# Convolution half of the output product on scaled fp16 parts: raw w_o rows, scales from squares

## The chip, the cores and the metric

The kernel runs on one core of a Trainium2 chip. A core has five engines that run their own instruction streams in order and meet at semaphores: TensorE (PE, matrix products), VectorE (DVE), ScalarE (ACT), GpSimd (POOL) and SyncE (SP). SP and POOL also issue the transfers (DMA) between the memory of the chip and the core; POOL's queue may convert or add on the way, SP's copies. The metric is the device time of one execution in microseconds (us).

## The reference

The program computes a two-layer encoder trunk on a sequence of 1024 rows of width 1024. Each layer has a mixer and a feed-forward part, each behind an RMS norm with a residual around it. The mixer has two halves of width 512, which one output matrix joins:

```python
h = _rmsnorm(x, g_mix[l])
p = h @ w_in[l]
...
y_att = softmax(q k / sqrt(96)) v          # 8 heads of 64, keys of 64 + 32 (rotary)
...
u = a * sigmoid(g)                          # gated half, 512 channels
u = silu(_layernorm(_dwconv(u, w_dw_conv, b_dw_conv), g_conv_ln, b_conv_ln))   # 31 taps
x = x + concatenate([y_att, u]) @ w_o[l]
...
x = x + gated_conv_ffn(_rmsnorm(x, g_ffn[l]), w_up[l], w_down[l])
```

The block is shortened from the reference; what matters here is the product with `w_o`. Its first half takes the attention output, its second half the output of the convolution module.

## The kernel before

Everything is held transposed: channels on the 128 partitions, the 1024 rows along the free axis, in two column halves of 512. To keep float32 precision, each operand of a product is split into an upper and a lower part (names end in `h` and `l`), and three matmuls per block (upper by upper, upper by lower, lower by upper) are added up in PSUM. In the feed-forward part and in the attention the parts are f16; in the projections and in the product with `w_o` they are float32r.

A layer runs in this order on PE:

- **Projection** (`project`). Sections of the product with `w_in` (`pg`, `pa` for the gated half, `pkv`, `pq`, `pkr`), then keys, queries and values. Beside it DVE works on the 31 taps of the convolution (`conv`, L1993), ACT on the gate sigmoids (L646), on copies for weights (`complete`, L200) and on products `far` for taps that a transfer adds up (L1999). A planner with a table of section times keeps a clock; `launch`, `work` and `supply` place evictions, taps and weight loads along it, and that fixes the order of each engine. `supply` loads a weight with a converting transfer on POOL's queue (the upper part), lets ACT write its negative (`complete`), and lets a second transfer add the source to it, which leaves the lower part. In layer 0 the rotary tables are computed at the same time, written out by two transfers and read back by eight `cos` and eight `sin` transfers on SP's queue (L670).
- **Scales** (`weight_squares`, `scales`). Near the end of the projection ACT takes sums of squares of the value weights (`vsq`) and of the gains (`sc`, L916); one small matmul (`sc0p`) adds them over partitions, and ten small DVE operations make powers of two from them.
- **Attention** (`attention`). 64 steps, each with scores `s`, exponentials `p` on ACT, a transposition `t`, the split `pt` (upper on ACT, lower on DVE) and the product `o`. An agenda, a list of functions by step number, adds other work: taps that are left (on ACT and POOL), the loads of the w_o tiles for the attention half from step 55 (`WO_AT`), the totals `lns` of the layer norm on POOL (from step `TOTAL_TIME`), the multiplies of `yt` by the softmax reciprocals (`LAST_MULT`, `Y_DELAY`), and the splits `ys` of the attention output (`ys_5l` on POOL).
- **Output product** (`wo_steps`, L1000). First `po<-ys`, the attention half, then `po<-us`, the convolution half; each is 8 blocks of output by 2 column halves by 4 tiles by 3 matmuls. `put(step, rank, f)` places loads, copies and evictions by step and by rank within it. The tiles of both halves come by converting and adding transfers on POOL's queue, 256 KB each. Layer norm and SiLU of the convolution run beside the first half; `close` (ACT) and `rest` (DVE) make the parts `us`. DVE adds the sums from PSUM to the residual (L1034, L1038).
- **Feed-forward part** (L1266, L1511), which the change does not touch.

Tiles come from pools of equal slots: 31 named `b`, 8 `m`, 3 `wr`, 8 `ws`. A load into a slot waits until the slot's last reader is done.

Of the kernel before, what the change touches and what calls it, by code (L numbers as in the profile page):

```python
# [9 lines left out]
F32 = mybir.dt.float32  # L10
F32R = mybir.dt.float32r
I32 = mybir.dt.int32
# [53 lines left out]
TOTAL_TIME = 59  # L66
Y_DELAY = 6
Y_LAST = 4
LAST_MULT = (60, 61)
WO_AT = 55  # L70
END_TURNS = 1
P_SCALE = 32768.0
# [64 lines left out]
class Encoder:  # L137
# [274 lines left out]
    def first_sections(self, l, supply):  # L412
# [14 lines left out]
        nc.scalar.activation(out=self.cp.tile([128, 1], F32, name="table"), in_=self.ones[:, 0:1], func=AF.Square)  # L427
# [83 lines left out]
        nc.gpsimd.tensor_copy(out=self.cp.tile([128, 1], F32, name="held"), in_=x[2][:, 0:1])  # L511
# [46 lines left out]
    def project(self, l, carry):  # L558
# [10 lines left out]
        qk = self.cp.tile([128, 8], F32, name=f"qk{l}", tag="qk", bufs=1)  # L569
        col = lambda i, n=1: qk[:, i:i + n]  # L570
# [290 lines left out]
        scales = {1: lambda: st.update(squares=self.weight_squares(l, w["v"])),  # L861
                  2: lambda: (st.update(scale=self.scales(l, st.pop("squares"))), score_scale())}
# [8 lines left out]
        coming, turning = list(starts.items()) + [("v", t + 6.0)], []  # L871
# [12 lines left out]
        gain_squares()  # L884
        launch(gate(0), -3)
# [21 lines left out]
        return u, conv, away, (qd, qrd, kd, krd), (kvs, w["v"], st["scale"]), heads  # L907

    def weight_squares(self, l, w):
        nc, par = self.nc, self.par[l]  # L910
        f = self.cp.tile([128, 20], F32, name=f"sc{l}", tag="sc", bufs=1)
# [4 lines left out]
        nc.scalar.activation(out=f[:, 8:16], in_=par[:, P_GFFN:P_GFFN + 8], func=AF.Square, accum_out=f[:, 2:3])  # L916
        return f
# [8 lines left out]
    def scales(self, l, f):  # L926
        nc = self.nc
        ps = self.bank(f"sc{l}p", (128, 3))
        nc.tensor.matmul(ps, self.ones, f[:, 0:3], start=True, stop=True)
        col = lambda i: f[:, i:i + 1]  # L930
        nc.vector.tensor_copy(out=f[:, 2:5], in_=ps)
        nc.vector.tensor_tensor(out=col(3), in0=col(2), in1=col(3), op=ALU.add)
        self.half_exponent(f[:, 5:7], f[:, 3:5])
        self.power(col(0), col(5), -1.0, 200.0)
        self.power(col(1), col(5), 1.0, 39.0)
        self.power(col(7), col(6), -1.0, 197.0)
        nc.vector.tensor_scalar(out=col(16).bitcast(I32), in0=col(6).bitcast(I32), scalar1=EXPONENT, scalar2=-20.0 * EXPONENT,
                                op0=ALU.mult, op1=ALU.add)
        nc.vector.tensor_copy(out=col(17), in_=col(16).bitcast(I32))
        nc.vector.tensor_scalar(out=f[:, 8:16], in0=self.par[l][:, P_GFFN:P_GFFN + 8], scalar1=col(7), scalar2=None, op0=ALU.mult)  # L940
        nc.vector.tensor_scalar(out=col(18), in0=col(17), scalar1=-2.0 ** 31, scalar2=None, op0=ALU.add)
        self.gs, self.back, self.nback = f[:, 8:16], col(17), col(18)
        return col(0), col(1)

    def layer(self, l, carry):
        with self.psum(f"mix{l}", ([f"w{i}" for i in range(3)], 1), 2):
            mixed = self.project(l, carry)
        with self.psum(f"attn{l}", 2, 4):
            casts, ready = {}, {}
            ahead = {WO_AT: lambda: [casts.update({m: self.wo_cast(l, m, 1)}) for m in range(4)],  # L950
                     **{58 + m: lambda m=m: ready.update({(1, m): self.complete(*casts.pop(m))}) for m in range(3)},
                     61: lambda: (ready.update({(1, 3): self.complete(*casts.pop(3))}), [casts.update({m: self.wo_cast(l, m, 1)}) for m in range(4, 8)])}
            begun = {"x": {}, "po": {}}
            begun["turn"] = lambda: ready.update({(1, m): self.complete(*casts.pop(m)) for m in range(4, 4 + END_TURNS)})
            conv, ys = mixed[1], self.attention(l, *mixed, ahead, ready, begun)
        with self.psum(f"ffn{l}", 0, ([f"d{i}" for i in range(8)], 1)):
            return self.feed(l, conv, ys, ready, casts, begun["x"])()

    def cast_pair(self, src, name, tag):
# [3 lines left out]
        return (hi, lo), hi, lo, src  # L963

# [37 lines left out]
    def wo_steps(self, l, conv, ys, w, casts, x, steps, put):  # L1002
# [11 lines left out]
        def cast(part, m):  # L1014
            casts[part, m] = self.wo_cast(l, m, part)

        def turn(part, m):
            w[part, m] = self.complete(*casts.pop((part, m)))

# [718 lines left out]
    def attention(self, l, u, conv, away, spill, kvs, loaded, ahead, wo, begun):  # L1738
# [7 lines left out]
        def rows(tt):  # L1746
            (kv, wv, _), ts = kvs, slice(tt * 128, (tt + 1) * 128)
# [107 lines left out]
        def sums(h, main, st, y, rb):  # L1855
# [9 lines left out]
            elif h % 2:  # L1865
                agenda[h * 8 + 10 + Y_DELAY].append(lambda: nc.gpsimd.tensor_tensor(out=y, in0=y, in1=rb, op=ALU.mult))
                agenda[h * 8 + 10 + Y_DELAY + (Y_DELAY if h < 5 else Y_LAST)].append(
# [39 lines left out]
        for i, (j, t) in enumerate(late):  # L1907
            n = max(int(SIDE_TIME * sum(costs[:i]) / sum(costs)), kinds[i] != "act")
# [120 lines left out]
    def conv_norm(self, l, conv, out, put):  # L2029
# [34 lines left out]
        def close(j, c):  # L2064
            if c == 0:
                out.append([self.blk(f"us{l}_{j}{i}", F32R) for i in "hl"])
            nc.scalar.copy(out=out[j][0][:, HALVES[c]], in_=st[j, "z"][:, HALVES[c]])

        def rest(j, c):
            hi, lo = (t[:, HALVES[c]] for t in out[j])  # L2070
            nc.vector.tensor_tensor(out=lo, in0=st[j, "z"][:, HALVES[c]], in1=hi.bitcast(F32), op=ALU.subtract)
# [84 lines left out]
```

## Time and profile before

| | us |
|---|---|
| median of 3 runs | 2216.79 (2216.55 to 2217.12) |
| profiled execution | 2216.41 |
| its span | 2214.6 |
| PE busy | 2200.9 (99%) |
| DVE busy | 1862.7 (84%) |
| ACT busy | 1485.7 (67%) |
| POOL busy | 592.8 (27%) |
| projection of layer 0, to the small matmul of the scales | 0 to 193.4 |
| attention of layer 0, from there to the output product | 193.4 to 415.6 |
| output product of layer 0 | 415.6 to 500.8 |

The granted clock of PE is 1.0 throughout. In the rows below, the first number is the start in us after the span's start and the second the duration of the row's instructions (with `xN`, of N instructions one after the other). In brackets stands how long the engine was idle before it and what it waited for. Rows of groups end with busy us, mean ns of one, and idle us before. L numbers are lines of the kernel before.

### The profile page before, as it was taken

The numbers are of one execution on the slowest core, as the hardware profiler recorded it, in microseconds if no ns is written. First come the engines' busy times: TensorE is split into PE (matmuls) and PEld (weight loads), VectorE is DVE, ScalarE is ACT, GpSimd is POOL, SyncE is SP. The second block draws the span as 40 slices with busy tenths as digits, with TensorE's granted clock in tenths as the row PEclk, the third lists the DMA queues.
The fourth block names the chain that finished last, engine by engine and source line by source line (L and its number), as shares of the span: only waits on it lengthen the run. The fifth ranks groups of instructions, "written<-read, shape, count | busy, mean of one in ns | idle before, by whom it ended". The sixth has DMA issues, their size and how long they took to land.

```text
span 2214.6 us, 29900 instructions
## 1 busy us (share of the span) xinstructions
PE 2200.9 (99%) x10774; PEld 1319.6 (60%) x10774; DVE 1862.7 (84%) x2644; ACT 1485.7 (67%) x2223; POOL 592.8 (27%) x546
## 2 busy tenths in 40 slices
PE   9999999999999999999999999999999999999998
PEld 8887666784444444644488876667744444446445
DVE  7989999868988887787859789997788888878877
ACT  5455988745888886554623669887468988865544
POOL 1221789511111111000012227974111111110000
PEclk9999999999999999999999999999999999999999
DMA  6886877955589886554558958779646888856533
GB/s 193 164 177 174 161 160 159 279 147 113 129 248 258 226 258 161 189 168 152 166 138 164 193 150 174 157 174 244 165 102 144 256 242 238 238 138 219 182 122 119
DMA packets 163269, 400.96 MB, mean 181 GB/s; under 512 B 22144, under 2 KB 30192, under 8 KB 163120
## 3 DMA queue, kind: packets, MB, share of 16 engines
q0 software_dynamic: 67136, 154.28, 37.7%
q1 hardware_dynamic: 95696, 244.24, 32.2%
q8 instruction: 84, 1.38, 0.3%
q10 hardware_dynamic: 288, 0.53, 0.1%
q14 instruction: 65, 0.53, 0.1%
HBM read 270.75 MB, written 69.66 MB: 154 GB/s over the span
## 4 chain that ended last, share of the span: by engine, by line
PE 90%; DVE 6%; ACT 3%; issue 1%; DMA 0%; DVEq 0%; ACTq 0%
PE p L1266 36%; PE pd L1511 17%; PE po L1000 7%; PE s L1775 6%; PE o L1839 4%; PE t L1816 4%; PE pa L237 2%; PE pg L237 2%; DVE conv L1993 2%; PE pg L555 2%; PE pq L237 1%; PE pkv L237 1%; PE pn L237 1%; PE pa L555 1%; PE pv L1751 1%
## 5 line engine op out<-in xcount | busy, mean ns | idle before, releaser
L1266 PE MATMUL p<-b,w 128*128 128x512 f16 x3696 | 804.0, 379 | 0.0
L1266 PEld LDWEIGHTS <-w 128*128 128x128 f16 x3696 | 361.3, 99 | 427.6 <-issue 1.1
L1511 PE MATMUL pd<-ab,wd 128*128 128x512 f16 (+2 forms) x1920 | 404.2, 373 | 0.0
L1157 POOL DMA_DIRECT2D wu<-in_w_up x176 | 152.6, 879 | 743.1 <-DVE w L1230 540.1
L1511 PEld LDWEIGHTS <-wd 128*128 128x128 f16 x1656 | 161.7, 98 | 179.6 <-issue 0.5
L1775 PE MATMUL s<-k,q 96*128 96x512 f16 x768 | 187.0, 379 | 0.0
L1230 DVE SCALAR_TENSOR_TENSOR w<-wu,wf,w 128x512 f16<-128x512 f32 (+1 forms) x216 | 177.1, 834 | 3.9 <-ACT w L1227 3.9
L1819 DVE SCALAR_TENSOR_TENSOR pt<-t,pt 128x512 f16<-128x512 f32 x256 | 163.6, 679 | 12.4 <-ACT pt L1818 9.2
L2010 POOL TENSOR_TENSOR late<-gate,par 128x1016 f32<-128x1016 f32 (+11 forms) x79 | 171.0, 2164 | 0.0
L1818 ACT ACTIVATE pt<-t 128x512 f16<-128x512 f32 x256 | 139.2, 596 | 42.8 <-PE t L1816 41.4
L1227 ACT ACTIVATE w<-wu,wf 128x512 f16<-128x512 f32 (+1 forms) x216 | 164.8, 781 | 0.0
L1786 ACT ACTIVATE p<-s,mx,qk 128x1024 f32<-128x1024 f32 x128 | 155.1, 1211 | 1.6 <-DVE mx L1778 0.6
L1777 DVE TENSOR_REDUCE mx<-s 128x1 f32<-128x1024 f32 x128 | 155.1, 1212 | 0.0
L1500 ACT ACTIVATE ab<-ac,ds 128x512 f16<-128x512 f32 x108 | 75.5, 716 | 108.6 <-DVE ac L1415 77.7
L1993 DVE SCALAR_TENSOR_TENSOR conv<-gate,par,conv 128x1009 f32<-128x1009 f32 (+14 forms) x110 | 139.8, 1274 | 3.3 <-ACT conv L655 0.6
L1816 PEld LDWEIGHTS t<-ident,p 128*128 128x128 f32 x1024 | 119.7, 141 | 29.1 <-ACT p L1786 2.1
L1816 PE MATMUL t<-ident,p 128*128 128x128 f32 x1024 | 134.4, 273 | 2.4 <-DVE yt L1846 1.2
L1839 PE MATMUL o<-pt,v 128*128 128x512 f16 x512 | 131.9, 379 | 1.2 <-DVE pt L1819 1.2
L1723 DVE SCALAR_TENSOR_TENSOR o<-zg,par,o 128x1023 f32<-128x1023 f32 x88 | 112.7, 1281 | 8.8 <-ACT o L1717 7.4
L1274 DVE SCALAR_TENSOR_TENSOR zg<-p,wf,zg 128x512 f32<-128x512 f32 x72 | 54.0, 751 | 72.0 <-PE p L1266 62.4
L1775 PEld LDWEIGHTS <-q 96*128 96x128 f16 x768 | 74.1, 97 | 64.5 <-issue 2.1
L1723 DVE SCALAR_TENSOR_TENSOR v<-zv,par,v 128x1023 f32<-128x1023 f32 x88 | 112.1, 1276 | 0.0
(2190 smaller groups left out, 3982.1 us busy)
## 6 DMA issues: line engine op xcount, KB each, us to landing
wu<-in_w_up SPq DMA_DIRECT2D x98, 512.0 KB
wu<-in_w_up POOLq DMA_DIRECT2D x176, 256.0 KB, 4.8
sd<-in_w_down SPq DMA_DIRECT2D x44, 512.0 KB
ws<-sd SPq DMA_DIRECT2D x44, 512.0 KB
act<-v SPq DMA_DIRECT2D x36, 512.0 KB
ac<-act SPq DMA_DIRECT2D x72, 256.0 KB
wo<-in_w_o POOLq DMA_DIRECT2D x64, 256.0 KB, 7.0
x_mix<-y SPq DMA_DIRECT2D x32, 256.0 KB
```

What stands on the lines that cost most here:

```text
L1227: nc.scalar.activation(out=t, in_=src, func=AF.Copy, scale=scale[f])
L1230: nc.vector.scalar_tensor_tensor(out=t, in0=src, scalar=scale[f], in1=hi, op0=ALU.mult, op1=ALU.subtract)
L1266: nc.tensor.matmul(ps, w[p][:, k * 128:(k + 1) * 128], b[:, q], start=(i in (1, 5, 2) and k == 0 and t == 0), stop=(k == 3 and t == 2), sk ...
L1511: nc.tensor.matmul(ps[t, m][:, cs], w[i, j][p][:, m * 128:(m + 1) * 128], b[:, q, cs], start=(i in (1, 5, 2) and j == 0 and s == 0), stop= ...
L1723: self.nc.vector.scalar_tensor_tensor(out=o[:, a:b], in0=z[:, at + a:at + b], scalar=self.par[l][:, tap:tap + 1], in1=o[:, a:b], op0=ALU.m ...
L1775: nc.tensor.matmul(ps[:, cs], q[0:96, i, qs], k[0:96, j, cs], start=(s == 0), stop=(s == 2))
L1777: nc.vector.tensor_reduce(out=mx, in_=ps, op=ALU.max, axis=AX.X, negate=True)
L1816: nc.tensor.transpose(tp[:, i, qi * 128:(qi + 1) * 128], st["p"][2 * qp + qi][:, kt * 128:(kt + 1) * 128], self.ident)
L1819: nc.vector.scalar_tensor_tensor(out=lo, in0=tp, scalar=P_SCALE, in1=hi, op0=ALU.mult, op1=ALU.subtract)
L1839: nc.tensor.matmul(po, v[2 * c + i][:, h // 2, e, :], pt[s][:, 2 * (c % 2) + i, :], start=(c == 0 and i == 0 and s == 0), stop=(c == 3 and ...
L1993: self.nc.vector.scalar_tensor_tensor(out=y[:, lo:hi], in0=u[:, lo + s:hi + s], scalar=self.tap(l, j, t), in1=y[:, lo:hi], op0=ALU.mult, o ...
L2010: self.nc.gpsimd.tensor_tensor(out=p[:, lo:hi], in0=u[:, lo + s:hi + s], in1=self.tap(l, j, t).broadcast_to([128, hi - lo]), op=ALU.mult)
```

## The change

Six edits go together.

1. The convolution half of the output product takes f16 parts instead of float32r. `close` and `rest` make `us` as f16 of the value times a power of two (`uscale`); the weights are f16 parts of w_o times another (`wscale`); `evict` multiplies the sum by the inverse of both (`uback`) as it adds it.
2. The weights of that half no longer come by converting and adding transfers on POOL's queue (8 + 8 per layer) with 8 ACT copies. Instead SP loads raw rows, four tiles of 512 KB per layer (`out_rows`, into `ws` slots), ACT makes the upper part (`upper`) and DVE the lower (`lower`), each 128x1024.
3. `wscale` comes from the sum of squares of the same rows: during the projection SP loads them once more into `b` slots, and ACT squares them in place (`out_squares`), four loads and four squares per layer, planned 16 us apart.
4. `uscale` comes from the squares of the layer norm's gain and bias. All gain squares now run ahead of the first gate (`gain_squares`). `scales` keeps five small DVE operations; twelve go into `more_scales` at attention step 4.
5. The planner asks for the value weight one microsecond earlier (`t + 5.0`), so its ACT copy (`wv0l`) stands before two casts of the queries.
6. Toward the end of the attention, the totals `lns` come two steps earlier, the last two multiplies of `yt` one step later, and the splits of the heads below 5 two steps later.

The core of the difference:

```diff
-TOTAL_TIME = 59
+TOTAL_TIME = 57
...
-LAST_MULT = (60, 61)
+Y_SPLIT = 8
+LATE_FROM = 0
+LAST_MULT = (61, 62)
...
+SCALES_AT = 4
+OUT_FROM, OUT_STEP, OUT_WAIT = 4.0, 20.0, 16.0
+WO_LOAD = (0, 1, 2, 3)
+WO_UPPER = (2, 2), (3, 2), (4, 2), (5, 2)
+WO_LOWER = (3, 2), (4, 2), (5, 2), (6, 2)
...
+        def out_squares(now):
+            while outs and outs[0][0] <= now:
+                at, i, t = outs.pop(0)
+                if t is None:
+                    outs.append((at + OUT_WAIT, i, self.out_rows(l, i, "b")))
+                    outs.sort(key=lambda e: e[0:2])
+                else:
+                    nc.scalar.activation(out=t, in_=t, func=AF.Square, accum_out=sc[:, 3 + i:4 + i])
...
-        coming, turning = list(starts.items()) + [("v", t + 6.0)], []
+        coming, turning = list(starts.items()) + [("v", t + 5.0)], []
...
         gain_squares()
+        self.gain_squares(l, sc)
...
             supply(clock["pe"])
+            out_squares(clock["pe"])
...
+    def more_scales(self, l, f):
+        nc = self.nc
+        col = lambda i: f[:, i:i + 1]
+        nc.vector.tensor_reduce(out=col(15), in_=f[:, 3:7], op=ALU.add, axis=AX.X)
+        nc.vector.tensor_tensor(out=col(16), in0=col(7), in1=col(8), op=ALU.add)
+        self.half_exponent(col(18), col(2))
+        self.half_exponent(f[:, 19:21], f[:, 15:17])
+        self.power(f[:, 27:29], f[:, 19:21], -1.0, 204.0)
+        self.power(f[:, 30:32], f[:, 19:21], 1.0, 50.0)
+        nc.vector.tensor_tensor(out=col(30), in0=col(30), in1=col(31), op=ALU.mult)
+        self.wscale, self.uscale, self.uback = (col(i) for i in (27, 28, 30))
...
+            ahead[SCALES_AT] = lambda: self.more_scales(l, mixed[4][3])
...
+    def out_rows(self, l, i, tag):
+        t = self.tmp(tag, f"wor{l}_{i}{tag}", F32, (128, 2, 512))
+        self.nc.sync.dma_start(out=t, in_=self.a["w_o"][l, 2 * i:2 * i + 2, :, HALVES[1]].rearrange("m p c -> p m c"))
+        return t
...
+        def upper(i):
+            t = self.tmp("ws", f"wo{l}_0{i}", F16, (128, 2, 2, 512))
+            nc.scalar.activation(out=t[:, :, 0], in_=casts[i], func=AF.Copy, scale=self.wscale)
...
+        def lower(i):
+            t = half.pop(("wo", i))
+            nc.vector.scalar_tensor_tensor(out=t[:, :, 1], in0=casts.pop(i), scalar=self.wscale, in1=t[:, :, 0],
+                                           op0=ALU.mult, op1=ALU.subtract)
...
-        for m in range(8):
-            put(m // 4, 5, lambda m=m: cast(0, m))
-            put(2 + m // 4, 2, lambda m=m: turn(0, m))
+        for i in range(4):
+            put(WO_LOAD[i], 5, lambda i=i: load(i))
+            put(*WO_UPPER[i], lambda i=i: upper(i))
+            put(*WO_LOWER[i], lambda i=i: lower(i))
...
-            nc.vector.tensor_tensor(out=xm, in0=ps.pop((c, m)), in1=xm, op=ALU.add)
+            nc.vector.scalar_tensor_tensor(out=xm, in0=ps.pop((c, m)), scalar=self.uback, in1=xm, op0=ALU.mult, op1=ALU.add)
...
-                out.append([self.blk(f"us{l}_{j}{i}", F32R) for i in "hl"])
-            nc.scalar.copy(out=out[j][0][:, HALVES[c]], in_=st[j, "z"][:, HALVES[c]])
+                t = self.blk(f"us{l}_{j}", F16, (128, 2, T))
+                out.append([t[:, i] for i in range(2)])
+            nc.scalar.activation(out=out[j][0][:, HALVES[c]], in_=st[j, "z"][:, HALVES[c]], func=AF.Copy, scale=self.uscale)
```

How the instructions stand on the engines, at three places. First ACT in the projection of layer 0, from the copy for `wkv10` on; `far` are tap products, `gate` is the gate of the fourth group of channels. Before:

```order
L200 ACTIVATE wkv10l<-wkv10h 128x1024
L1999 ACTIVATE far_0_12_779<-gate_0_416,par_63 128x1021
L1999 ACTIVATE far_2_16_782<-gate_2_631,par_63 128x1023
L646 ACT_TABLE_LOAD
L646 ACTIVATE gate_3_786<-gate_3_786 128x1024
```

Now, with the square of the second pair of w_o rows (`wor_1b`) in place:

```order
L207 ACTIVATE wkv10l<-wkv10h 128x1024
L594 ACTIVATE wor_1b,sc_85<-wor_1b 128x1024
L2052 ACTIVATE far_0_12_789<-gate_0_420,par_63 128x1021
L2052 ACTIVATE far_2_16_792<-gate_2_638,par_63 128x1023
L664 ACT_TABLE_LOAD
L664 ACTIVATE gate_3_796<-gate_3_796 128x1024
```

The square stands ahead of the `far` products, the table load and the gate sigmoid. Its load is on SP's queue; this is the queue around it in layer 0, now:

```order
L1002 DMA wor_0b<-in_w_o 128x2x512
L338 DMA freq<-in_freq 128x2
L352 DMA rope<-in_positions 128x128
L400 DMA rope_tables<-rope 128x128 x2
L688 DMA cos_647<-rope_tables 16x1024 x8
L688 DMA sin_648<-rope_tables 16x1024 x8
L1002 DMA wor_1b<-in_w_o 128x2x512
L1002 DMA wor_2b<-in_w_o 128x2x512
L1002 DMA wor_3b<-in_w_o 128x2x512
```

The first load goes ahead of the rotary tables, the other three behind them. Second, POOL toward the end of the attention of layer 0; `yt` is a head pair's output, `lns` the total over the convolution's channels, `ys_5l` the lower part of the third head pair. Before:

```order
L1866 TENSOR_TENSOR yt_4_3007<-yt_4_3007,rb_4_3008 128x1024
L201 DMA wo_10_3731<-in_w_o 128x512
L201 DMA wo_11_3733<-in_w_o 128x512
L2021 TENSOR_TENSOR lns_3877<-conv_0_475,conv_1_539 128x1024
L201 DMA wo_12_3735<-in_w_o 128x512
L2021 TENSOR_TENSOR lns_3877<-lns_3877,conv_2_717 128x1024
L221 TENSOR_TENSOR ys_5l<-yt_4_3007,ys_5h 128x1024
```

Now:

```order
L1919 TENSOR_TENSOR yt_4_3028<-yt_4_3028,rb_4_3029 128x1024
L2074 TENSOR_TENSOR lns_3832<-conv_0_479,conv_1_545 128x1024
L208 DMA wo_10_3752<-in_w_o 128x512
L2074 TENSOR_TENSOR lns_3832<-lns_3832,conv_2_726 128x1024
L208 DMA wo_11_3754<-in_w_o 128x512
L2074 TENSOR_TENSOR lns_3832<-lns_3832,conv_3_866 128x1024
L208 DMA wo_12_3756<-in_w_o 128x512
L228 TENSOR_TENSOR ys_5l<-yt_4_3028,ys_5h 128x1024
```

All three totals now stand ahead of `ys_5l`; before, one came after it. Third, DVE at attention step 4, with `more_scales` (names `sc`) between the row maxima `mx` and the split `pt`; this is part of what stands there now:

```order
L969 TENSOR_TENSOR sc_85<-sc_85 128x1
L942 TENSOR_SCALAR sc_85<-sc_85 128x1
L972 TENSOR_SCALAR sc_85<-sc_85 128x1
L974 CAST sc_85<-sc_85 128x1
L975 TENSOR_SCALAR sc_85<-par_63,sc_85 128x8
L976 TENSOR_SCALAR sc_85<-sc_85 128x1
L1872 SCALAR_TENSOR_TENSOR pt_10_1898<-t_0_20_1892,pt_00_1897 128x2x256
L1872 SCALAR_TENSOR_TENSOR pt_10_1898<-t_0_21_1903,pt_00_1897 128x2x256
```

Before, the two `pt` rows stood right behind the row maxima; the twelve small operations are ahead of them now.

More of the change, by code (lines that the diff above doesn't have):

```diff
@@ L426, in first_sections @@
             nc.tensor.matmul(warm, self.ones, self.ones, start=True, stop=True)
-        nc.scalar.activation(out=self.cp.tile([128, 1], F32, name="table"), in_=self.ones[:, 0:1], func=AF.Square)
+        nc.scalar.activation(out=self.cp.tile([128, 1], F32, name="table", tag="table", bufs=1), in_=self.ones[:, 0:1], func=AF.Square)
         def load(i, c):
@@ L510, in first_sections @@
             nc.tensor.matmul(ps[i][:, c], w[i][p][:, 0:128], hl[0][q][:, c], start=p + q == 0, stop=False)
-        nc.gpsimd.tensor_copy(out=self.cp.tile([128, 1], F32, name="held"), in_=x[2][:, 0:1])
+        nc.gpsimd.tensor_copy(out=self.cp.tile([128, 1], F32, name="table2", tag="table", bufs=1), in_=x[2][:, 0:1])
         order = [(1, i) for i in range(3)] + [(k, i) for k in range(2, 8) for i in range(3)]
@@ L569, in project @@
         qk = self.cp.tile([128, 8], F32, name=f"qk{l}", tag="qk", bufs=1)
+        sc = self.cp.tile([128, 32], F32, name=f"sc{l}", tag="sc", bufs=1)
+        outs = [(OUT_FROM + OUT_STEP * i, i, None) for i in range(4)]
         col = lambda i, n=1: qk[:, i:i + n]
@@ L906, in project, with weight_squares @@
         work(1e9)
-        return u, conv, away, (qd, qrd, kd, krd), (kvs, w["v"], st["scale"]), heads
-    def weight_squares(self, l, w):
+        return u, conv, away, (qd, qrd, kd, krd), (kvs, w["v"], st["scale"], sc), heads
+    def weight_squares(self, l, w, f):
         nc, par = self.nc, self.par[l]
-        f = self.cp.tile([128, 20], F32, name=f"sc{l}", tag="sc", bufs=1)
         for k in range(2):
@@ L1746, in rows @@
         def rows(tt):
-            (kv, wv, _), ts = kvs, slice(tt * 128, (tt + 1) * 128)
+            (kv, wv), ts = kvs[0:2], slice(tt * 128, (tt + 1) * 128)
             ps = self.bank(f"pv{l}_{tt}")
```

52 lines of the change are left out of this document (29 added, 23 removed).

## The prediction

> **What bounds the kernel now.** I read busy time by engine, then the chain of work that ended last, then what PE (the matrix engine) waited for.
>
> ```profile
> PE 2200.9 (99%) x10774; PEld 1319.6 (60%) x10774; DVE 1862.7 (84%) x2644; ACT 1485.7 (67%) x2223; POOL 592.8 (27%) x546
> ...
> PE 90%; DVE 6%; ACT 3%; issue 1%; DMA 0%; DVEq 0%; ACTq 0%
> ```
> ```profile
> PE t L1816 <- DVE yt L1846: 1.2, 2, 0.6
> PE o L1839 <- DVE pt L1819: 1.2, 4, 0.3
> ...
> PE sc0p L929 <- ACT sc L916: 0.8, 1, 0.8
> ...
> PE po_e L1000 <- POOL ys_5l L221: 0.2, 1, 0.2
> ```
>
> PE works in 99% of the span and its named waits are a few tenths each. So two things count: PE work that becomes shorter, and any step that makes PE wait where it does not now. Such a wait is paid in full, as no idle time is left to swallow it. The sum stands against the profiled execution (2216.41 us, span 2214.6 and 1.8 around it), 0.4 below the median of the runs.
>
> **Part 1, the matmuls.** The convolution half holds 2 layers x 2 column halves x 8 blocks x 12 = 384 matmuls. They go from float32r to f16. Rows of the chain give both pitches, for the same 128x512 shape:
>
> ```profile
> 415.71 16.33 PE po L1000 x72
> ...
> 512.40 36.26 PE p L1266 x168
> ```
>
> 16.33 / 72 = 0.2268 us against 36.26 / 168 = 0.2158. 384 x 0.0110 = **4.2 us saved**, all on PE's path. PE hides its weight loads (1319.6 busy beside 2200.9), so nothing comes from smaller weights.
>
> **Part 2, squares of w_o rows inside the projection (layer 0).** SP gets four 512 KB loads, ACT four squares of 128x1024. Squares 3 and 4 wait for nothing; the first costs ACT about a microsecond ahead of a gate. The second stands in ACT between the `wkv10l` copy and the `far` products, and its load stands in SP behind all cos and sin loads.
>
> ```profile
> 73.53 5.51 SPq L670 DMA_DIRECT2D cos<-rope_tables  x8
> 79.08 6.06 SPq L670 DMA_DIRECT2D sin<-rope_tables  x8
> ```
> ```profile
> 83.46 1.06 ACT L200 ACTIVATE wkv10l<-wkv10h 128x1024 fp32r<-128x1024 f32 x1 [7.97 <-PE pg L237]
> 84.43 2.17 ACT L1999 ACTIVATE far<-gate,par 128x1021 f32<-128x1021 f32 x2
> 86.62 1.28 ACT L646 ACT_TABLE_LOAD   x1
> 87.92 1.06 ACT L646 ACTIVATE gate<-gate 128x1024 f32<-128x1024 f32 x1
> ```
>
> The last sin load is issued by 79.08 + 6.06 = 85.1, so the w_o load leaves then, after ACT is ready for it (84.4). If it lands at time L, the square (1.06, as the copy of the same size in the first row) ends at L + 1.06, and `far`, table load and gate sigmoid come D = L + 1.06 - 84.43 later. DVE waits for that sigmoid:
>
> ```profile
> 89.01 1.22 DVE L648 TENSOR_TENSOR gate<-gate,rx 128x1024 f32<-128x1024 f32 x1 [0.94 <-ACT gate L646]
> ...
> 143.80 1.29 DVE L747 SCALAR_TENSOR_TENSOR cqs_0l<-cq,par,cqs_0h 128x1024 fp32r<-128x1024 f32 x1 [3.37 <-ACT cqs_0h L745]
> ...
> 156.81 1.27 DVE L747 SCALAR_TENSOR_TENSOR kvs_0l<-ckv,par,kvs_0h 128x1024 fp32r<-128x1024 f32 x1
> ```
> ```profile
> 90.00:140.00 50.00, 50.00 (x226) 41.49 (x225) 48.99 (x46) 19.76 (x22) 13.75 (x16) 1.00 0.89 180
> ```
> ```profile
> 131.78 1.05 ACT L723 COPY krt<-krt 32x1024 f32<-32x1024 f32 x1 [6.20 <-DVE krt L720]
> ```
> ```profile
> 159.66 0.61 PE L237 MATMUL pk<-kvs_0l,wk0h 128*128 128x512 f32 x2
> ```
>
> DVE is busy 48.99 of 50 us from 90 to 140 (the third busy figure of the row), so it cannot catch up. Its idle 3.37 us at 143.80 end with ACT work which itself waits for DVE (131.78 row), so they move along. PE needs `kvs_0l` at 159.66; DVE ends it at 158.08. PE therefore loses D - 1.6. Behind the waiting square stand also the POOL transfers of `far` products and wkr; their users come later on the same delayed DVE, or PE tens of microseconds on.
>
> How late is L? No row shows this load. Bounds, from the queues and from 512 KB transfers between 70 and 100 us (last column: us from issue to landing):
>
> ```profile
> q0 software_dynamic: 67136, 154.28, 37.7%
> q1 hardware_dynamic: 95696, 244.24, 32.2%
> ```
> ```profile
> wkv10l<-in_w_in POOLq DMA_DIRECT2D x1, 512.0 KB, 5.7
> wq00h<-in_w_in POOLq DMA_DIRECT2D x1, 512.0 KB, 10.4
> ```
>
> SP's queue (q1) took 0.322 x 2214.6 / 244.24 = 2.92 us of all 16 engines per MB, so 1.5 for this load, POOL's (q0) 0.377 x 2214.6 / 154.28 = 5.4 per MB: L is 86.6 at the earliest. As slow as `wkv10l`, and with its own 1.5 behind that one (issued at 84.8), it lands at 92.3. I take 90: next to the `wkv10l` row, issued in the same microsecond, but on the queue that needs half the engine time per byte. Then D = 6.6 and **PE loses 5.0 us**; the ends give 1.6 and 7.3. In layer 1 the tables are already there and nothing blocks SP: 0.
>
> The Trainium skill (DMA: Bandwidth & Descriptors, section Anatomy of one DMA — SWDGE (gpsimd) path) fits a transfer as 2.0 us plus its bytes at 436 GB/s; by that estimate the load lands at 88.3, PE loses 3.3 and the sum is 1.7 us lower. The 5.7 and 10.4 of the rows above say that this stretch is not that free.
>
> **Part 3, end of attention.** POOL's `lns` totals come two steps earlier, the last multiply one step later.
>
> ```profile
> 397.49 0.94 DVE L1864 SCALAR_TENSOR_TENSOR yt<-yt,rb 64x512 f32<-64x512 f32 x1
> ...
> 401.02 2.98 DVE L1864 SCALAR_TENSOR_TENSOR yt<-yt,rb 64x512 f32<-64x512 f32 x1
> ```
> ```profile
> 400.62 2.83 POOL L221 TENSOR_TENSOR ys_5l<-yt,ys_5h 128x1024 fp32r<-128x1024 f32 x1
> ```
> ```profile
> 403.50 0.50 PE L1000 MATMUL po_e<-ys_5l,wo 128*128 128x512 f32 x1 [0.17 <-POOL ys_5l L221]
> ...
> 404.85 1.38 PE L1816 MATMUL t<-ident,p 128*128 128x128 f32 x8 [0.61 <-DVE yt L1846]
> ```
>
> The second multiply takes 2.98 instead of 0.94 while `ys_5l` runs, and PE then waits 0.17 + 0.61. With the totals out of the way `ys_5l` starts behind its ACT half, some two us earlier, and the multiply stands behind the next steps. I take 0.7 of the 0.78 per layer: **-1.4** (bounds 0 and -1.6).
>
> **Part 4, scales.** The wait at sc0p (0.8) ends with the gain square in ACT, which now stands at the start of the layer, and `wv0l` goes earlier. DVE is next, so I take **-0.5** (0 to -0.8). The twelve small operations of `more_scales` run in attention step 4. Ten like them took 195.46 + 0.15 - 194.29 = 1.3:
>
> ```profile
> 194.29 0.15 DVE L931 COPY sc<-sc0p 128x3 f32<-128x3 f32 x1
> ...
> 195.46 0.15 DVE L941 TENSOR_SCALAR sc<-sc 128x1 f32<-128x1 f32 x1
> ```
> ```profile
> 225.19 1.29 DVE L1819 SCALAR_TENSOR_TENSOR pt<-t,pt 128x512 f16<-128x512 f32 x2 [0.27 <-ACT pt L1818]
> ...
> 228.22 1.29 DVE L1819 SCALAR_TENSOR_TENSOR pt<-t,pt 128x512 f16<-128x512 f32 x2 [0.36 <-ACT pt L1818]
> ...
> 231.21 0.74 DVE L1846 SCALAR_TENSOR_TENSOR yt<-o,sc,yt 64x512 f32<-64x512 f32 x1 [0.32 <-ACT yt L1845]
> ```
>
> So about 1.5 us, of which 0.27 + 0.36 + 0.32 of idle time takes up most before step 5, where PE already waits for `pt` (second row of the waits). I take 0.5 per layer: **+1.0** (0 to 2 x 1.5).
>
> **Part 5, the output stage.** POOL loses 32 issues, ACT 16 copies; SP gets eight loads, ACT eight `upper` and DVE eight `lower`, four of each per layer. The evictions and the `us` halves change their operation, not their size or count, so I cost them at nothing.
>
> ```profile
> 432.52 1.29 DVE L287 TENSOR_REDUCE lnr0v<-lnr0t 128x4 f32<-128x512 f32 x2 [3.67 <-PE lnr0t L276]
> ...
> 438.87 2.72 DVE L2060 SCALAR_TENSOR_TENSOR conv<-conv,par,lnr0s 128x512 f32<-128x512 f32 x4 [2.45 <-PE lnr0s L314]
> ...
> 448.01 0.69 DVE L2071 TENSOR_TENSOR us_0l<-lnsg,us_0h 128x512 fp32r<-128x512 f32 x1
> ...
> 455.78 0.17 DVE L1178 TENSOR_REDUCE wt<-wt 128x4 f32<-128x8 f32 x1 [4.08 <-PE wt L1189]
> ...
> 459.55 1.28 DVE L1230 SCALAR_TENSOR_TENSOR w<-wu,wt,w 128x1024 f16<-128x1024 f32 x1 [1.74 <-ACT w L1227]
> ```
>
> ```profile
> 450.24 0.39 PE L1000 MATMUL po<-us_0l,wo 128*128 128x512 f32 x1
> ```
>
> A `lower` has the tile of the 459.55 row, 1.28 us. DVE is idle 3.67, 2.45 and 4.08 us there, so the 5.1 us of four fit. One of them between the scalings makes `us_0l` late by 1.3, and PE reads that at 450.24, 1.5 after its end at 448.70. The raw rows leave SP among the w_up loads of this stage, where an issue waits for a free slot; the first leaves at the stage's start, and PE needs the convolution half last, so I see cover of tens of microseconds. **0** then, and up to +1 over both layers; were those idle stretches gone, it would be 5 per layer.
>
> Sum: -4.2 + 5.0 - 1.4 - 0.5 + 1.0 + 0 = **-0.1**, so 2216.3 us. With every bound low, -4.2 + 1.6 - 1.6 - 0.8 = -5.0 (2211.4); with every bound high, -4.2 + 7.3 + 3.0 + 1.0 = +7.1 (2223.5).
>
> **Rivals.**
> - *The load is hidden.* If it leaves SP before the tables, or DVE makes D good before `kvs_0l`, the 5.0 falls away: 2211.3. For it: D of 1.6 or less is free. Against it: the order in SP, and DVE's 48.99 of 50.
> - *The load lands much later (slower).* PE's loss is L - 85.0; from L = 94.5 the kernel is over 0.2% slower. Three w_o loads leave SP together beside the software queue, where `wq00h` took 10.4: landing at 85.1 + 10.4 = 95.5 costs 10.5, 2221.8.
> - *The collision moves.* The first multiply, one step later, now meets the earlier `ys_5l` and takes 2.98 in turn; the 1.4 of part 3 is lost: 2217.7. The rows 0.94 and 2.98 speak for it, the room behind `ys_5l` against it. The Trainium skill (SBUF — State Buffer, section Who interferes with whom) says that a DVE operation with two SBUF inputs and a reading POOL operation exclude each other for the whole instruction; the 2.98 agrees.
>
> **Numbers.** A change within 0.2% (4.4 us) is about what a measurement of this kernel cannot tell from none. Chances: the forecast with a stall of 3 to 7 us 0.40, moved collision 0.12, both nearly always within 0.2% (0.02 faster, 0.04 slower); hidden load 0.25, of which 0.21 faster; late load, with part 4 at its bound, 0.23, of which 0.22 slower. Faster 0.23, same 0.51, slower 0.26. The likeliest case alone spans 2213 to 2219; the range over the cases is 2210.5 to 2223.
>
> **What would show it.** `po<-us` rows of f16 at a pitch near 0.216; ACT idle some 5 us ahead of a square, with a w_o load as releaser, near 84 us; DVE's `gate` multiply near 95 instead of 89; PE waiting for `kvs_0l` near 160 by about 5 us, and not in layer 1; the waits of `ys_5l` and `yt` gone; `pt` waits of about 0.5 in attention step 5. I am wrong if that square waits for nothing, or if PE waits for a w_o tile in the output stage.

## The result, and the profile after

| | before | after |
|---|---|---|
| median of 20 runs, us | 2216.82 | 2220.03 |
| lowest to highest, us | 2216.55 to 2217.61 | 2217.72 to 2222.53 |
| profiled execution, us | 2216.41 | 2219.01 |
| its span, us | 2214.6 | 2217.2 |

The ratio is 1.0014 (95% interval 1.0008 to 1.0020). The change makes the kernel slower by 3.2 us, and its time now varies over 4.8 us from run to run, where it varied over 1.1. The spread goes with PE's granted clock, averaged over each run: the four runs at 0.999 took 2217.72 to 2219.23 us, the eleven at 0.998 took 2219.00 to 2220.83, the five at 0.997 took 2221.14 to 2222.53.

The list of PE's waits after the change shows two long ones that were not there, `t` for `pt` and `pk` for `kvs_0l`. The wait at `kt` is longer, and those of `t` for `yt` (1.2 before) and of `o` for `pt` (1.2 in four before) are shorter; sc0p and ys_5l are gone. After each name stand the sum in us, the number of waits and the longest:

```profile
PE t L1869 <- DVE pt L1872: 4.1, 2, 3.4
PE pk L244 <- DVE kvs_0l L765: 1.4, 1, 1.4
PE kt L603 <- ACT rkv L709: 1.4, 2, 1.1
...
PE t L1869 <- DVE yt L1899: 0.5, 2, 0.3
...
PE o L1892 <- DVE pt L1872: 0.2, 1, 0.2
```

The row of `kt` before:

```profile
PE kt L585 <- ACT rkv L691: 0.5, 2, 0.2
```

Both programs issue the same 10774 matmuls on PE in the same order, so the starts of one matmul in both traces can be subtracted. This ledger, in us after the start of each span, says where time is lost and won; "here" is the change of the difference since the row above. It is of the two profiled executions, which are 2.6 us apart, and not of the medians.

| matmul | before | after | difference | here |
|---|---|---|---|---|
| projection, before `kt` (layer 0) | 146.99 | 147.43 | +0.44 | +0.44 |
| last before `sc0p` | 192.17 | 195.52 | +3.35 | +2.9 |
| `sc0p` | 193.41 | 195.80 | +2.40 | -0.95 |
| attention, before step 5 | 227.29 | 229.66 | +2.38 | 0 |
| attention, after step 5 | 232.61 | 236.76 | +4.15 | +1.8 |
| behind the second wait of `o` for `pt` of before (356) | 356.21 | 359.29 | +3.09 | -1.1 |
| end of the attention | 408.41 | 410.70 | +2.29 | -0.8 |
| first of the feed-forward part | 502.57 | 502.60 | +0.03 | -2.3 |
| layer 1, attention, before step 5 | 1325.37 | 1325.59 | +0.22 | +0.2 |
| after step 5 | 1328.40 | 1334.99 | +6.59 | +6.4 |
| behind the waits of `o` for `pt` of before | 1454.17 | 1459.85 | +5.68 | -0.9 |
| end of the attention | 1507.64 | 1512.57 | +4.93 | -0.75 |
| first of the feed-forward part | 1602.39 | 1605.11 | +2.71 | -2.2 |

So the product itself wins 2.2 to 2.3 us per layer. The row group of its matmuls after the change, all in f16:

```profile
L1040 PE MATMUL po<-us,wo 128*128 128x512 f16 x384 | 84.2, 379 | 0.5 <-DVE wt L1231 0.5
```

Two things lose: the square in the projection (2.9) and, far more, attention step 4 (1.8 and 6.4). ACT and SP around the square, after the change:

```profile
83.95 0.42 SPq L1002 DMA_DIRECT2D wor_1b<-in_w_o  x1
```
```profile
83.89 1.06 ACT L207 ACTIVATE wkv10l<-wkv10h 128x1024 fp32r<-128x1024 f32 x1 [7.97 <-PE pg L244]
87.74 1.06 ACT L594 ACTIVATE wor_1b<-wor_1b 128x1024 f32<-128x1024 f32 x1 [2.79 <-DMA wor_1b<-in_w_o]
...
92.29 1.06 ACT L664 ACTIVATE gate<-gate 128x1024 f32<-128x1024 f32 x1
```
```profile
93.38 1.23 DVE L666 TENSOR_TENSOR gate<-gate,rx 128x1024 f32<-128x1024 f32 x1 [4.89 <-ACT gate L664]
```

ACT waits 2.79 us for the rows, and DVE, which was idle for 0.94 us ahead of its `gate` multiply before the change, is idle for 4.89. The load took 3.8 us from issue (83.95) to the square (87.74).

Attention step 4, DVE's small operations in layer 1 with POOL's work at that time:

```profile
1323.15 0.15 DVE L963 TENSOR_REDUCE sc<-sc 128x1 f32<-128x4 f32 x1
1323.21 1.34 DVE L964 TENSOR_TENSOR sc<-sc 128x1 f32<-128x1 f32 x1
1324.47 0.28 DVE L946 TENSOR_SCALAR sc<-sc 128x1 int32<-128x1 int32 x2
...
1325.38 0.15 DVE L974 CAST sc<-sc 128x1 f32<-128x1 int32 x1
1325.45 3.08 DVE L975 TENSOR_SCALAR sc<-par,sc 128x8 f32<-128x8 f32 x1
```
```profile
1322.34 2.18 POOL L2063 TENSOR_TENSOR late<-gate,par 128x1019 f32<-128x1019 f32 x1
...
1325.97 2.53 POOL L2063 TENSOR_TENSOR late<-gate,par 128x1021 f32<-128x1021 f32 x1
```

Two operations on one and on eight columns, which take 0.16 and 0.22 us elsewhere, last 1.34 and 3.08. The first ends at 1324.55, POOL's tap product at 1324.52; the second ends at 1328.53, the next product at 1328.50. The second starts 0.52 us before that product's row, while POOL still issues a transfer. The issuing alone does not hold such an operation: in layer 0 the same one stands beside an issue (229.64, POOL's issue from 229.56 to 230.48) and takes 0.22. What held it for that half microsecond, the trace does not show. In layer 0 the same sum of two columns takes 1.46 and ends with a product (226.52 + 2.20 = 228.72):

```profile
227.28 1.46 DVE L964 TENSOR_TENSOR sc<-sc 128x1 f32<-128x1 f32 x1
```
```profile
226.52 2.20 POOL L2063 TENSOR_TENSOR late<-gate,par 128x1019 f32<-128x1019 f32 x1
```

And PE in layer 1, then its granted clock (the column before the last two) in stretches of 4 us:

```profile
1323.10 1.46 PE L1828 MATMUL s<-k,q 96*128 96x512 f16 x6
...
1329.24 1.12 PE L1869 MATMUL t<-ident,p 128*128 128x128 f32 x4 [3.38 <-DVE pt L1872]
1330.15 2.77 PE L1828 MATMUL s<-k,q 96*128 96x512 f16 x6
```
```profile
1322.00:1326.00 4.00, 3.86 (x24) 2.38 (x22) 3.86 (x13) 3.69 (x9) 3.70 (x5) 1.00 0.70 132
1326.00:1330.00 4.00, 0.76 (x4) 0.76 (x5) 4.00 (x5) 0.50 (x1) 2.50 (x2) 0.76 1.04 196
1330.00:1334.00 4.00, 4.00 (x12) 1.47 (x11) 3.42 (x5) 2.50 (x4) 1.90 (x1) 0.50 0.35 65
1334.00:1338.00 4.00, 4.00 (x23) 2.64 (x22) 3.01 (x6) 3.07 (x5) 3.70 (x4) 0.89 0.60 114
```

PE is idle 3.38 us and then works at half its clock: six `s` matmuls take 2.77 us, which took 1.46 just before. About 3.4 of the 6.4 us are the wait, 3.0 the clock.

### The profile page after: what moved, and what is told of

It is laid out like the page before. It is cut to its first block, busy times and chain, and to the rows that moved or that the text cites. A ratio compares the mean times of both kernels' runs of the same rounds, so it can differ in the third digit from the quotient of the medians.

```text
span 2217.2 us, 29912 instructions
## 1 busy us (share of the span) xinstructions
PE 2199.9 (99%) x10774; PEld 1287.5 (58%) x10774; DVE 1876.5 (85%) x2666; ACT 1498.2 (68%) x2239; POOL 569.4 (26%) x514
## 4 chain that ended last, share of the span: by engine, by line
PE 90%; DVE 6%; ACT 2%; DMA 1%; issue 1%; SPq 0%; POOL 0%; DVEq 0%; ACTq 0%
PE p L1319 36%; PE pd L1564 17%; PE po L1040 7%; PE s L1828 6%; PE o L1892 4%; PE t L1869 4%; PE pa L244 2%; DVE conv L2046 2%; PE pg L562 2%; PE pn L244 1%; PE pq L244 1%; PE pg L244 1%; PE pkv L244 1%; PE pa L562 1%; PE pv L1804 1%; PE pk L244 1%
```

## The experiments

**The small operations at another place.** `more_scales` moves from attention step 4 to the end of the attention, where POOL only issues transfers.

```diff
-            ahead[SCALES_AT] = lambda: self.more_scales(l, mixed[4][3])
...
-            begun["turn"] = lambda: ready.update(...)
+            begun["turn"] = lambda: (ready.update(...), self.more_scales(l, mixed[4][3]))
```

> The changed kernel with the twelve small DVE operations of more_scales moved from attention step 4 to the end of the attention, where POOL computes nothing. Theory 1 (two of the small operations wait for a POOL product that reads the same memory port, 1.75 us of PE time in layer 0 and 6.6 in layer 1 by the two traces): about 8 us under the profiled run of the changed kernel, so 2211 to 2212, the pt waits near 230 and 1326 us gone, and a spread of the runs of about 1 us instead of 5. Rival 1 (the DVE time of twelve operations is what costs, wherever they stand): 2217 to 2219 and PE waits at the end of the attention instead.

Measured: 2211.95 (2210.25 to 2212.98), ratio to the kernel before 0.9978 (0.9969 to 0.9987). That is 8.1 us less than the changed kernel, and the predicted places are clean: the two rows that lasted 1.34 and 3.08 now read, at the end of the attention of layer 0,

```profile
413.10 0.15 DVE L964 TENSOR_TENSOR sc<-sc 128x1 f32<-128x1 f32 x1
...
414.20 0.22 DVE L975 TENSOR_SCALAR sc<-par,sc 128x8 f32<-128x8 f32 x1
```

Rival 1 falls: the twelve operations are still there, and take 0.14 to 0.22 each in both layers. The spread did not shrink to 1 us, but to 2.7; the stalled square is still in this kernel.

**The row loads earlier.** In the changed kernel the four loads are planned 20 us apart, and each square 16 us behind its load. Here all four loads are asked for at once, ahead of the rotary tables; the squares keep their places.

```diff
-        outs = [(OUT_FROM + OUT_STEP * i, i, None) for i in range(4)]
+        outs = [(OUT_FROM, i, None) for i in range(4)]
...
-                    outs.append((at + OUT_WAIT, i, self.out_rows(l, i, "b")))
+                    outs.append((at + OUT_WAIT + OUT_STEP * i, i, self.out_rows(l, i, "b")))
```

> The changed kernel with all four w_o row loads of the projection asked for at once, in layer 0 ahead of the rotary tables in SP's queue; the squares stay where they are. Theory (the square waits for a load that stands behind the table transfers): ACT no longer waits near 84 us, PE's waits at kt and kvs_0l fall back to 0.24 and 0, 3.0 us less than the changed kernel, about 2217, with the wide spread still there. Rival (the 1.5 MB themselves slow the weight transfers of the projection): the stall moves to other waits and the time stays at 2219 to 2220.

Measured: 2214.79 (2213.47 to 2216.38), ratio 0.9991 (0.9982 to 1.0000), 5.2 under the changed kernel. The waits at kvs_0l and the long one at kt are gone. Between the profiled executions the gain is 2.6 (2219.01 and 2216.38), near the 3.0 expected. Between the medians it is twice that, and how long each stall is in the runs without a trace was not seen.

**Both.**

> Both edits of the two runs before. If the two causes are separate, their gains add: 2219.0 - 8.3 - 3.0 and about 0.5 for the small operations at their new place, 2208 to 2209.5, faster than the kernel before by 0.3 to 0.4%. If one hides the other, 2211 or more.

Measured: 2207.68 (2207.48 to 2207.97), ratio 0.9959 (0.9947 to 0.9972), slightly below the 2208 to 2209.5 expected. The two causes are separate: the gains of the two profiled executions, 8.3 and 2.6, add up to 10.9, and together they gave 11.0. This version is faster than both kernels. Its five runs lie within 0.5 us: the spread of the changed kernel came from the two stalls. ACT's square now follows the copy directly:

```profile
83.98 1.06 ACT L207 ACTIVATE wkv10l<-wkv10h 128x1024 fp32r<-128x1024 f32 x1 [7.97 <-PE pg L244]
84.95 1.05 ACT L594 ACTIVATE wor_1b<-wor_1b 128x1024 f32<-128x1024 f32 x1
```

**Which operations wait for POOL.** Single small operations in the kernel before, in every fourth attention step. Their results are not used.

```diff
+        pair = lambda: nc.vector.tensor_tensor(out=p[:, 16:17], in0=g[:, 0:1], in1=g[:, 1:2], op=ALU.add)
+        wide = lambda: nc.vector.tensor_scalar(out=p[:, 2:8], in0=g[:, 0:6], scalar1=g[:, 8:9], scalar2=None, op0=ALU.mult)
+        total = lambda: nc.vector.tensor_reduce(out=p[:, 19:20], in_=g[:, 0:8], op=ALU.add, axis=AX.X)
+        one = lambda: nc.vector.tensor_scalar(out=p[:, 2:3], in0=g[:, 0:1], scalar1=2.0, scalar2=None, op0=ALU.mult)
+        a, b = (pair, wide) if l == 0 else (total, one)
+        return {9 + 4 * i: (a, b)[i % 2] for i in range(10)}
```

> The kernel before with one small DVE operation added in every fourth attention step from 9 on: in layer 0 in turn a sum of two columns from memory and a product of six columns with a factor; in layer 1 in turn a sum over eight columns of one operand and a product of a single column with a constant. Theory 1: where a POOL product runs, the sum of two columns lasts until that product ends (1 to 2.5 us instead of 0.16); the sum over one operand stays at 0.15 to 0.2 everywhere; of the products with a factor it is open, and the run tells which of them wait. Rival 1 (DVE's own load): every probe takes 0.15 to 0.3.

The one execution took 2222.56 us. Durations (ns, lowest/median/highest of five each): `pair`, `wide`, `total`, `one` in this order.

```profile
L964 DVE TENSOR_TENSOR sc<-par x5: 148/150/4596, 240.8 to 341.1; 128x1 f32<-128x1 f32 x5
```
```profile
L965 DVE TENSOR_SCALAR sc<-par x5: 220/912/2101, 253.4 to 357.4; 128x6 f32<-128x6 f32 x5
```
```profile
L966 DVE TENSOR_REDUCE sc<-par x5: 150/152/155, 1344.0 to 1442.7; 128x1 f32<-128x8 f32 x5
```
```profile
L967 DVE TENSOR_SCALAR sc<-par x5: 143/144/145, 1357.0 to 1455.2; 128x1 f32<-128x1 f32 x5
```

The slowest `pair` and `wide`, and a `one` in the middle of a POOL product:

```profile
278.12 2.10 DVE L965 TENSOR_SCALAR sc<-par 128x6 f32<-128x6 f32 x1
...
341.09 4.60 DVE L964 TENSOR_TENSOR sc<-par 128x1 f32<-128x1 f32 x1
...
1455.15 0.14 DVE L967 TENSOR_SCALAR sc<-par 128x1 f32<-128x1 f32 x1
```
```profile
277.85 2.33 POOL L2025 TENSOR_TENSOR conv<-conv,late 128x1016 f32<-128x1016 f32 x1 [4.23 <-DMA conv<-late]
...
341.18 2.66 POOL L1878 TENSOR_TENSOR yt<-yt,rb 128x1024 f32<-128x1024 f32 x1
343.50 2.16 POOL L2022 TENSOR_TENSOR late<-gate,par 128x1011 f32<-128x1011 f32 x1
...
1454.43 2.32 POOL L2025 TENSOR_TENSOR conv<-conv,late 128x1010 f32<-128x1010 f32 x1
```

A product of two operands in POOL holds up DVE's sum of two columns and its scaling of six, until the product ends (280.22 against 280.18; 345.69 against 345.66, two products in a row). A reduction over one operand and a scaling of one column pass beside it. The shortest `pair` and `wide` (0.15 and 0.22) met no product, or one in its last 0.1 us. A single small operation held DVE for 4.6 us, and PE was idle for 2.43 us behind it.

**Step 4 with operations that do not wait.** The kernel with early rows, `more_scales` left at step 4, the sum of two columns as a reduction, two products on ACT.

```diff
-        nc.vector.tensor_tensor(out=col(16), in0=col(7), in1=col(8), op=ALU.add)
+        nc.vector.tensor_reduce(out=col(16), in_=f[:, 7:9], op=ALU.add, axis=AX.X)
...
-        nc.vector.tensor_tensor(out=col(30), in0=col(30), in1=col(31), op=ALU.mult)
+        nc.scalar.activation(out=col(30), in_=col(30), func=AF.Copy, scale=col(31))
...
-        nc.vector.tensor_scalar(out=f[:, 3:11], in0=self.par[l][:, P_GFFN:P_GFFN + 8], scalar1=col(23), scalar2=None, op0=ALU.mult)
+        nc.scalar.activation(out=f[:, 3:11], in_=self.par[l][:, P_GFFN:P_GFFN + 8], func=AF.Copy, scale=col(23))
```

> The kernel with early w_o rows, more_scales left at attention step 4, but three of its operations changed: the sum of two columns is taken by a reduction over one operand, and the two products (of two columns, and of eight gains with a factor) go to ACT. Theory 1 (the wait is for POOL's product, by operations with two operands from memory or with a factor over several columns): none of the small operations lasts over 0.3 us, PE loses only what 1.2 us of DVE time cost there, at most 1.0 over both layers, so 2208 to 2209 against 2207.7 with the operations at the end of the attention and 2214.8 with the old operations at step 4. Rival 1 (DVE time or the place itself): 2213 to 2215.

Measured: 2212.17 (2211.70 to 2212.72), between the two theories. The trace says why: the next operation in line now waits.

```profile
224.22 0.14 DVE L964 TENSOR_REDUCE sc<-sc 128x1 f32<-128x2 f32 x1
224.29 1.40 DVE L946 TENSOR_SCALAR sc<-sc 128x1 int32<-128x1 int32 x2
```
```profile
223.46 2.20 POOL L2063 TENSOR_TENSOR late<-gate,par 128x1019 f32<-128x1019 f32 x1
```

The row holds two operations; the first covers one column, the second two, and it is the second that ends with POOL's product (225.69 against 225.66). So I took the two-column operations apart.

```diff
-        self.half_exponent(f[:, 19:21], f[:, 15:17])
-        self.power(f[:, 27:29], f[:, 19:21], -1.0, 204.0)
-        self.power(f[:, 30:32], f[:, 19:21], 1.0, 50.0)
+        for e in range(2):
+            self.half_exponent(col(19 + e), col(15 + e))
+        for e in range(2):
+            self.power(col(27 + e), col(19 + e), -1.0, 204.0)
+            self.power(col(30 + e), col(19 + e), 1.0, 50.0)
```

> The run e5_one_operand again, with the four operations over two columns taken apart into eight over one column each. In e5 the reduction over two columns and the operation over one column lasted 0.145, but the next one, over two columns, lasted 1.29 and ended with POOL's product. Theory, mended (an operation with a factor waits for POOL's product if it covers two or more columns, and not if it covers one): none lasts over 0.2 us, the waits of t for pt (0.9 and 0.7) go, and the time is 2208 to 2209.5, the rest above 2207.7 being DVE time of some 1.5 us. Rival (any operation with a factor may wait, by chance of its moment): some still last over 1 us and the time stays near 2212.

Measured: 2209.99 (2209.54 to 2210.35). No small operation lasts over 0.16 us, though in both layers all of them stand beside one POOL product. The rest above 2207.68, 2.3 us, is more than expected: by the ledger of the two traces PE loses 1.1 us at step 4 in each layer. That is what the bare work, thirteen operations on DVE and two on ACT, costs there.

**The end of the attention.** On the version with both causes removed, first the splits back at their old step, then the totals and multiplies.

```diff
-Y_SPLIT = 8
+Y_SPLIT = 6
```

> The kernel with both causes removed (2207.7) and the splits of the heads below 5 back at their old step (Y_SPLIT 6 instead of 8). By the traces the waits of o for pt near 307 and 356 us (0.3 each) and their like in layer 1 went away with the later split: with it back, 1.9 us slower, 2209.6. If they went away for another reason (less transfer traffic on POOL), 2207.7.

```diff
-TOTAL_TIME = 57
+TOTAL_TIME = 59
...
-LAST_MULT = (61, 62)
+LAST_MULT = (60, 61)
```

> The kernel with both causes removed and the order at the end of the attention back (TOTAL_TIME 59, LAST_MULT 60 and 61), Y_SPLIT left at 8. Theory of the prediction (the second multiply waits for ys_5l): 0.8 us per layer back, 2209.3. Rival (the waits stay away since POOL no longer issues 16 transfers there): 2207.7.

Measured: 2209.54 (2208.99 to 2210.07), 1.9 slower, and 2209.26 (2209.05 to 2209.36), 1.6 slower. The old waits come back, in the first run and in the second, and both rivals fall:

```profile
PE o L1891 <- DVE pt L1871: 1.2, 4, 0.3
```
```profile
PE t L1868 <- DVE yt L1898: 1.2, 2, 0.6
...
PE po_e L1039 <- POOL ys_5l L228: 0.2, 1, 0.2
```

**What a wait of PE costs beyond itself.** The kernel before with 1 to 10 extra DVE reductions at ten attention steps; their results are not used.

```diff
+            for _ in range(n):
+                nc.vector.tensor_reduce(out=p, in_=u, op=ALU.max, axis=AX.X)
+        return {12 + 8 * i: lambda i=i: more(i + 1 + 5 * l) for i in range(5)}
```

> The kernel before with extra reductions of 128x1024 (1.2 us each, one operand) in DVE at attention steps 12, 20, 28, 36 and 44: 1 to 5 of them in layer 0, 6 to 10 in layer 1. It asks what an idle time of PE costs beyond itself. Theory: PE's clock falls once it was idle for longer than some time between 2.4 us (the idle time after the slowest probe, clock 1.00 afterwards) and 3.4 us (layer 1 of the changed kernel, 0.50 afterwards), and stays down for a few us; idle times under it cost only themselves. Rival: the fall to 0.50 in the changed kernel was by chance, and the clock stays at 1.00 here.

The one execution took 2288.40 us. From two reductions on, PE's idle times were 1.04, 2.13, 3.38, 4.65, 6.24, 7.32, 8.41, 9.66 and 10.91 us. Behind 1.04 the clock stayed at 1.00. Behind 2.13 it fell, here with the stretch that holds the idle time and the one after it:

```profile
306.54 1.23 PE L1826 MATMUL t<-ident,p 128*128 128x128 f32 x8 [2.13 <-DVE rs L1869]
```
```profile
304.18:307.59 3.41, 1.28 (x11) 0.91 (x10) 3.38 (x6) 0.35 (x1) 3.11 (x3) 1.00 0.91 171
307.59:311.00 3.41, 3.41 (x11) 1.21 (x9) 3.21 (x6) 2.72 (x5) 3.11 (x3) 0.50 0.94 175
```

The longest wait did no more harm afterwards than the others. The clock was at 0.50 behind it, for 4.5 us:

```profile
1518.20:1520.20 2.00, 2.00 (x9) 1.85 (x10) 2.00 (x3) 0.60 (x1) 0.00 (x0) 0.50 0.05 10
```

The rival falls: every idle time from 3.38 on is followed by 3.1 to 5.4 us at 0.50. The span is 72.0 us longer than that of the kernel before, and the idle times make 53.8 of it, so about 2 us per fall (eight of them) are left for the clock. But the boundary I named falls as well. In the run with the single small operations, an idle time of 2.43 us was followed by 1.00:

```profile
346.34 0.66 PE L1828 MATMUL t<-ident,p 128*128 128x128 f32 x4 [2.43 <-DVE pt L1831]
```
```profile
341.47:344.89 3.42, 2.44 (x14) 1.18 (x11) 3.42 (x1) 2.99 (x6) 3.42 (x2) 1.00 0.82 151
344.89:348.30 3.41, 1.96 (x11) 1.17 (x12) 3.37 (x6) 0.60 (x1) 3.11 (x3) 1.00 0.30 57
348.30:351.71 3.41, 2.58 (x16) 1.58 (x15) 3.37 (x6) 2.38 (x5) 3.11 (x3) 1.00 0.93 173
```

So between 2.1 and 3.4 us the length alone does not decide, and the traces show what does. In each of the eleven traces the granted clock changes only at times that lie whole multiples of 3.41 us apart; the stretches of 3.41 and 3.42 us in the tables above are cut there. The 2.13 us lie whole in one stretch, of which PE works 1.28 us. The 2.43 us are divided, 0.98 in one stretch and 1.45 in the next. Over all eleven traces, the ends of the programs included, no stretch with up to 1.90 us of idle time was followed by a fall, and every one with 1.94 or more was. Once down, the clock came back behind stretches with 0.27 us of idle time or less and stayed down behind those with 0.74 or more. In layer 1 of the changed kernel 2.23 of the 3.38 us lie in one stretch; the clock is at 0.50 from 1328.09 to 1334.92, and PE works 5.68 us of that time. Half of it, 2.8 us, is nearly all of the 3.0 put down to the clock above. Whether all matmuls count as work alike was not tried.

## Why the prediction was wrong

It forecast 2216.3, a change of -0.1, and the change is +3.2. The time lies inside the range, for another reason than the prediction gives. The prediction also took a change within 0.2% for one that a measurement cannot tell from none; this one, 0.14%, is clear of none by its interval. Term by term, from the ledger of the profiled executions:

| step | predicted | measured |
|---|---|---|
| matmuls (part 1) | -4.2 | -4.5 |
| square in the projection (part 2) | +5.0 | +2.9 |
| end of the attention (part 3) | -1.4 | -1.55 |
| `Y_SPLIT` | not costed | -2.0 |
| sc0p (part 4) | -0.5 | -0.95 |
| `more_scales` (part 4) | +1.0, at most 3.0 | +8.1 |
| output stage (part 5) | 0 | nothing seen |

The measured terms add up to 2.0; the 0.44 and 0.2 of the other rows of the ledger make it 2.6.

**The step that failed is "So about 1.5 us, of which 0.27 + 0.36 + 0.32 of idle time takes up most"** in part 4. It priced the twelve operations by their durations at the end of the projection (0.15 to 0.22 each), where POOL computed nothing. At step 4 POOL computes tap products most of the time, and two of the twelve last until such a product ends. In layer 1 this made PE idle for 3.38 us, and the clock's fall made 6.4 of it. By the medians of the runs with and without the move the term is 7.1 to 8.1. The bound of 3.0 held only for the work itself, which the run with single columns measured: 1.1 per layer instead of my 0.5. A rule for the sum of two columns stood in the prediction, with the rival of the moved collision (The Trainium skill, SBUF — State Buffer, section Who interferes with whom), and with it a row, the multiply of 2.98 us; I applied it there to a tile of 64x512 and not to single columns. The scaling of eight columns, which cost most, has one tile and a factor, and the words quoted there do not cover it. That the size of the operation has no part in it is what the 4.60 us of one column show.

**Part 2 had the mechanism right, and its size was too large in the profiled execution only.** The chain (SP's queue, ACT, the gate sigmoid, DVE without idle time, kvs_0l) came out at each of its places; a part of the loss fell on `kt`, which the prediction did not name. The formula holds too: the square ended at 88.80, ACT was ready for it at 84.86, so D = 3.9 and D - 1.6 = 2.4; PE's waits at kt and kvs_0l grew by 0.88 and 1.41, together 2.3, and another 0.5 came behind them. What was mis-sized there is the landing. The load was issued 1.2 us earlier than I had it (83.95) and took 3.8 us instead of 4.9. That is nearer to the 3.2 us estimated in the prediction by the Trainium skill (DMA: Bandwidth & Descriptors, section Anatomy of one DMA — SWDGE (gpsimd) path), which fits transfers issued by GpSimd, than to the 5.7 of the software queue's row. By the medians the square costs 4.3 (without the stall of step 4) to 5.2 us (with it), so the 5.0 forecast fits the usual run; what is longer in those runs, no trace shows.

**Parts 1, 3 and 5 held.** f16 has the pitch of the row I took it from, 0.216 us from one matmul's start to the next. The end of the attention gained what its two waits had cost, though the one for `yt` only shrank, from 0.6 to 0.3; the run with the old order gave the gain back (1.6). The moved collision did not come: the first multiply took 0.67 us in the changed kernel. The wait at sc0p gave 0.95, more than its bound of 0.8. I overlooked that the later split of the early heads takes away four waits of `o` for `pt`, although their row, 1.2 us in four, stood second among my quotations; with 1.9 us by its own run it is worth more than the end of the attention.

In the profiled execution the two errors, 7.1 too little and 2.1 too much, and the overlooked 2.0 cancel in part. That the sum came near is luck, and its sign is wrong.

## What to carry to other kernels

Price a small VectorE operation by what GpSimd does at that moment: with two operands from memory, or a factor over two or more columns, it can cost the rest of a GpSimd product, however few its elements are; a reduction or a single column passes. Put such bookkeeping where GpSimd only issues transfers, or write it in the forms that pass. And where a kernel's bound is the matrix engine, follow each wait to its length: one that took more than 1.9 us of a stretch of 3.41 also brought the clock down here. That cost 1.6 to 3 us more (half of the time that PE worked at 0.50), whether the wait was 2 us long or 11.

## What the runs showed of the hardware

- The operations that wait have two operands from memory (one column: up to 4.60 us) or a factor over two, six or eight columns (up to 1.29, 2.10 and 3.08). One column with a factor (0.14) and a reduction (0.15) never did: in five cases each, four of them beside a POOL product, and in all of the run with single columns. The Trainium skill agrees, though I had not thought of so few columns: VectorE: DVE Perf Modes, section Mode 2×_2P — use both read ports for one tensor, has a one-source operation read its tile through both ports where the outermost dimension longer than one is even, or odd and the same in source and result. Two, six and eight columns have such a dimension, and a single column has none; that the use of both ports is what collides, no run here shows by itself.
- PE's clock fell to 0.50 behind an idle time of 2.13 us and not behind one of 2.43, and behind all of 3.38 and more. It changes on a grid of 3.41 us, and it fell behind each stretch of the grid with 1.94 us of idle time or more and behind none with 1.90 or less. The Trainium skill (TensorE: Matmul & The Clock Gate, section Part 1: The HAM clock gate) speaks of an idle window of about 3.4 us that runs freely. The length and the free run agree with the traces. A window in which PE never works is not needed: one with 1.28 us of work sufficed.
- The spread from run to run was 4.8 us with both stalls (20 runs), 2.7 and 2.9 with one of them (11 runs each) and 0.5 with none (5 runs). With both it went with the granted clock of the run, from 0.999 to 0.997.
